# Splitting a weight block earlier, pinning its casts, and storing one output block in two parts, in a Strassen-Winograd MLP

## The chip, the cores and the metric

One core of a Trainium2 chip. The metric is the device time of one execution in microseconds (us). A kernel is quoted by the median of its timed executions; two kernels are compared by a ratio of executions made in the same rounds on the same chip. One profiled execution of each kernel gives its trace. That one execution need not be a median one.

The engines are named as in the profile: PE (matmul), PEld (weight load), DVE (VectorE), ACT (ScalarE), POOL (GpSimd) and SP (SyncE, which issues most of the DMAs).

## The reference

```python
# x: (8, 1024, 1024) f32, w1: (1024, 4096) f32, w2: (4096, 1024) f32
def reference(x, w1, w2):
    h = x @ w1
    h = 0.5 * h * (1 + np.tanh(np.sqrt(2 / np.pi) * (h + 0.044715 * h ** 3)))
    return (h @ w2).astype(np.float32)
```

## The kernel before

The 8192 rows of x go through in eight blocks of 1024 rows. Each block has a first product (x by w1, then gelu) and a second product (by w2). Both are done by Winograd's form of Strassen's algorithm: matrices are cut into quarters named 11, 12, 21, 22, and seven products of sums of quarters replace eight. All matmuls are f16, accumulated in f32. From the third block on ("steady" blocks) Strassen is applied twice for the second product, and for part of the first. The first two blocks apply it once, and use the time to make what the others need: the first block casts w1 and w2 from f32 to f16 and stores them to HBM, the second one makes the sums of quarters of quarters ("splits") and stores them too.

So three places matter here. **The first block's second product**, where quarters of w2 arrive in f32, are cast and used at once:

```python
# matmul2_made(sb, ...): second product of the first two blocks (cut)
def late_copy(out, in_):                  # cast on ACT, ordered behind the last gelu
    with tc.issue_after(gelu_last[0].ins):
        nc.scalar.copy(out=out, in_=in_)
...
bring("11", pool_copy, False)             # load w2 quarter 11, cast on POOL
bring("21", pool_copy, False)
bring("12", late_copy, True)              # 8 loads of 512 KB, 8 casts of 128x1024 on ACT
keep("11")                                # store the f16 form to HBM for later blocks
bring("22", late_copy, True)
for b in ("21", "12", "22"):
    keep(b)
...
for m, name, first in ((1, "a", True), (2, "b", True), (5, "c", True), (6, "a", False),
                       (3, "c", False), (7, "a", False), (4, "a", False)):
    for q in range(NQ):
        ...
        matmuls2(bank, s2[q] if m == 6 else rows(g[operands[m]], q), pieces(m), first)
        post(m, q, bank)                  # ACT copies or DVE adds of the bank
        if (m, q) == (2, 1) and sb == 0:
            xb = x_cast(sb + 1, at[1])    # cast of the next x by DMA on POOL's queue
        if (m, q) == ((5, 0) if sb else (6, NQ - 1)):
            xs = XOps(x_transpose(xb, load_in_order))   # transposes by DMA on SP's queue
        ...
        run((m, q))                       # DVE jobs of the table FILL, in program order
```

The table `FILL[sb]` says after which product (key `mq`) which DVE job is put: `g` sums of gelu's output, `w` sums of w2 quarters, `p1n` one sum of the split of quarter 11, `x` sums of the next x.

```python
slots("""10:g60;11:g61;12:g62;13:g63
;20:g50 w50 w51;21:g51 w52;22:w53 g52;23:g53 ...
```

**The second block's first product.** Its eight iterations j are one long stream of matmuls. The splits of raw quarters of w2 are made in it, two iterations for each quarter; they load halves of a quarter into buffers of a pool of four (`gcp`, "gc" in the trace), sum, and store:

```python
SPLIT_IN_M1 = (1, 2, 3)                   # quarters 11, 21, 22, named as in bring
...
if sb == 1 and j < 2 * len(SPLIT_IN_M1):
    m, h = SPLIT_IN_M1[j // 2], j % 2
    splits = split_in_m1(m, h)
...
def split_jobs(m, pieces):                # the other way to split, with whole u buffers
    def make(n):
        u, op, v = W_SUM[n]
        t[n] = unit(NI // 2, OH // 2)
        for h in range(2):
            tt(t[n][:, h * QC:(h + 1) * QC, :], operand(u, h), operand(v, h), op, True)
        nc.gpsimd.dma_start(out=in_d[m][:, SUMS.index(n)], in_=t[n])
```

**The seam between two steady blocks.** In the last product of a block (table `FILL_2`) the output quarters are put together. Quarter 22 gets two additions on DVE (`v`, `y`) before it is stored, and the block's last job (`i3`) makes four "inner sums" of the next x:

```python
;71:w11 w12;72:w21 w22;73:a37;74:a36 y11;75:a35 y12;76:a33 y21;77:y22
;31:z11 z12;32:z21 z22;33:v11 v12;34:v21 v22;36:n6;37:n3 i3
...
elif kind == "v":
    add(7, 5, b)
    if b[1] == "2":
        store_rows(sb, "22", m - 1, into[7][m - 1])
...
# next block's first product, iteration j (cut)
for h in range(2):
    add(a[h], banks_b[h])                 # this add releases PE
if sb > 1 and j == 0 and 3 not in xs.inner:
    xs.make_inner(3)                      # four sums of 128x512 f16, where i3 didn't make them
```

## Time and profile before

| | before |
|---|---|
| median of 3 executions | 1510.43 us (1510.37 to 1510.51) |
| the traced execution | 1513.48 us, span 1511.7, mean granted clock 0.996 |
| start of the first block's second product | 117.29 us |
| first block's second product | 102.93 us |
| second block's first product | 103.31 us |
| second block's second product | 96.69 us |
| six steady blocks, to PE's end | 1086.86 us |

The stages are read from the timeline of PE: from the first matmul of a stage to the first of the next. 448 matmuls of 128x512 at 0.2158 us are 96.7 us, so the second block's second product runs at full rate, and 102.93 and 103.31 hold some 6 us each of holes and slow clock. The traced execution is 3.05 us longer than the median.

How to read the lines below. A hole is a stretch in which PE is idle. In a timeline a line is: start, length, engine, line of the kernel, operation, output and input, form, number of instructions; the bracket at its end is the idle time before it and what ended it. In the windows view the columns are the window, its length, busy time (instructions) of PE, PEld, DVE, ACT and POOL, then the granted PE clock (1.00 is full speed), the DMA share and GB/s. SPq is the queue of the DMAs that SP issues. The prediction below shows most of the view of before. Two windows that it only tells of are these; the third figure from the end is the clock:

```profile
152.00:156.00 4.00, 3.93 (x11) 1.49 (x11) 4.00 (x6) 0.59 (x1) 0.79 (x2) 0.57 1.16 353
284.00:288.00 4.00, 3.38 (x10) 1.32 (x10) 4.00 (x7) 3.40 (x7) 1.23 (x3) 0.65 0.50 201
```

In both, PE gets through only ten or eleven matmuls in 3.93 and 3.38 us of busy time; at the full rate these would hold some 18 and 16.

### The profile page before, as it was taken

What the parts mean: (1) busy time and instruction counts of PE and PEld (TensorE: products, weight loads), DVE (VectorE), ACT (ScalarE), POOL (GpSimd) and SP (SyncE); (2) the same over time, 40 slices, a digit from 0 to 9 for tenths busy, and PEclk for the clock granted to TensorE, in tenths of its full rate; (3) what the DMA queues carried; (4) which work ended last, traced back from release to release, by engine and by line L of the source; (5) the groups of instructions that cost most, each with busy time, mean ns of one, the idle gap of its engine ahead of it and who ended that gap; (6) DMA issues with size and microseconds to landing.
All of it is one profiled execution on the core that took longest, in us unless ns stands there. A gap on an engine that the chain in (4) does not pass through costs nothing.

```text
span 1511.7 us, 26283 instructions
## 1 busy us (share of the span) xinstructions
PE 1483.2 (98%) x9839; PEld 959.9 (63%) x9839; DVE 1164.9 (77%) x1820; ACT 616.1 (41%) x1157; POOL 228.1 (15%) x315
## 2 busy tenths in 40 slices
PE   7999999999999999999999999999999999999998
PEld 3444444444455688557875588655886568855687
DVE  6654647758757799778997699867998779977788
ACT  5665116541056511664126631366214662156510
POOL 5551123312311011010111000110001101001010
PEclk9999999999999999999999999999999999999999
DMA  9999797999797898989989899898989999897894
GB/s 320 354 333 401 192 333 246 338 355 287 291 344 193 306 288 299 340 217 353 294 304 334 203 371 302 292 317 246 336 267 324 309 271 315 267 353 246 299 280 177
DMA packets 240095, 449.51 MB, mean 297 GB/s; under 512 B 80608, under 2 KB 85728, under 8 KB 239072
## 3 DMA queue, kind: packets, MB, share of 16 engines
q1 hardware_dynamic: 216256, 360.79, 71.3%
q0 software_dynamic: 23712, 87.05, 18.7%
q8 instruction: 77, 1.26, 0.3%
q14 instruction: 50, 0.41, 0.1%
HBM read 357.56 MB, written 104.86 MB: 306 GB/s over the span
## 4 chain that ended last, share of the span: by engine, by line
PE 83%; DVE 7%; DMA 5%; issue 3%; POOL 1%; ACT 0%; SPq 0%; DVEq 0%; POOLq 0%
PE ps L397 42%; PE ps L857 30%; PE ps L898 11%; DVE u L120 6%; DMA u<-in_w_dram 1%; DMA raw_d<-u 1%; DVE tmp L120 1%; DMA in_d<-gc 1%; DMA u<-in_x_dram 1%; DMA gc<-raw_d 1%; DVE gc L120 0%; DMA out_dram<-tmp 0%; POOL in_d L806 0%; SPq L133 0%; POOL w_d L214 0%
## 5 line engine op out<-in xcount | busy, mean ns | idle before, releaser
L397 PE MATMUL ps<-u 128*128 128x512 f16 (+1 forms) x4160 | 764.1, 346 | 16.4 <-DVE tmp L120 12.1
L120 DVE TENSOR_TENSOR tmp<-tmp,ps 128x256 f32<-128x256 f32 (+1 forms) x936 | 454.0, 533 | 274.8 <-PE ps L397 162.0
L397 PEld LDWEIGHTS <-u 128*128 128x128 f16 x4160 | 407.0, 98 | 369.9 <-issue 27.0
L136 ACT COPY tmp<-ps 128x512 f32<-128x512 f32 x416 | 235.1, 581 | 324.3 <-PE ps L397 160.9
L410 ACT ACTIVATE g<-tmp 128x512 f16<-128x512 f32 x384 | 241.7, 633 | 175.9 <-DVE tmp L120 175.7
L857 PE MATMUL ps<-u,gc 128*128 128x256 f16 x2688 | 300.4, 273 | 0.0
L857 PEld LDWEIGHTS <-gc 128*128 128x128 f16 x2688 | 262.5, 98 | 31.2
L120 DVE TENSOR_TENSOR u<-u 128x512 f32<-128x512 f32 (+3 forms) x312 | 235.2, 797 | 14.6 <-DMA u<-raw_d 8.9
L857 PE MATMUL ps<-u,g 128*128 128x256 f16 x2016 | 227.9, 273 | 0.0
L136 ACT COPY u<-ps 128x512 f32<-128x512 f32 (+1 forms) x136 | 78.8, 586 | 346.1 <-PE ps L857 341.5
L857 PEld LDWEIGHTS <-g 128*128 128x128 f16 x2016 | 197.3, 98 | 24.7
L898 PE MATMUL ps<-u,g 128*128 128x512 f16 x768 | 168.7, 382 | 3.9 <-DVE u L120 3.8
L120 DVE TENSOR_TENSOR u<-u,ps 128x512 f32<-128x512 f32 x216 | 147.4, 685 | 24.1 <-PE ps L857 18.5
L647 POOL DMA_DIRECT2D out_dram<-u x58 | 48.8, 884 | 731.2 <-DVE u L120 305.6
L898 PEld LDWEIGHTS <-g 128*128 128x128 f16 x768 | 75.5, 98 | 96.5 <-issue 5.7
L120 DVE TENSOR_TENSOR g<-g,g 128x2048 f16<-128x2048 f16 (+1 forms) x136 | 131.0, 986 | 1.6 <-ACT g L410 1.6
L120 DVE TENSOR_TENSOR gc<-g,gc 128x2048 f16<-128x2048 f16 x84 | 102.6, 1221 | 1.0 <-DVE gc L120 0.5
L120 DVE TENSOR_TENSOR gc<-g 128x2048 f16<-128x2048 f16 x78 | 95.2, 1221 | 0.0
L410 ACT ACTIVATE g<-ps 128x512 f16<-128x512 f32 x128 | 76.5, 597 | 10.1 <-PE ps L397 6.9
L139 POOL CAST u<-gc 128x1024 f16<-128x1024 f32 x40 | 47.9, 1207 | 40.5 <-DMA gc<-in_w_dram 36.2
L635 POOL DMA_DIRECT2D out_dram<-tmp x32 | 17.6, 550 | 110.6 <-DVE tmp L120 91.6
L494 POOL TENSOR_TENSOR gc<-g 128x2048 f16<-128x2048 f16 x6 | 24.4, 4064 | 63.2 <-ACT g L410 63.2
(33 smaller groups left out, 226.7 us busy)
## 6 DMA issues: line engine op xcount, KB each, us to landing
u<-w_d SPq DMA_DIRECT2D x336, 256.0 KB, 6.1
u<-in_d SPq DMA_DIRECT2D x168, 512.0 KB, 7.0
u<-raw_d SPq DMA_DIRECT2D x252, 256.0 KB, 7.0
out_dram<-u POOLq DMA_DIRECT2D x58, 512.0 KB, 7.1
gc<-in_w_dram SPq DMA_DIRECT2D x48, 512.0 KB, 6.0
u<-in_d SPq DMA_DIRECT2D x96, 256.0 KB, 6.7
raw_d<-u SPq DMA_DIRECT2D x32, 512.0 KB, 9.9
u<-raw_d SPq DMA_DIRECT2D x32, 512.0 KB, 11.8
```

The source lines that it names most:

```text
L120: i = nc.vector.tensor_tensor(out=out, in0=in0, in1=in1, op=op)
L136: tc.keep_in_program_order(nc.scalar.copy(out=out, in_=in_))
L139: pool_last[0] = nc.gpsimd.tensor_copy(out=out, in_=in_)
L397: tc.keep_in_program_order(nc.tensor.matmul(bank, lhsT=w, rhs=x, start=first and k == 0, stop=k == n - 1, skip_group_check=not first,))
L410: gelu_last[0] = nc.scalar.activation(out=g[b][:, c, :], in_=src, func=GELU)
L494: nc.gpsimd.tensor_tensor(out=early[7], in0=u, in1=v, op=SUB)
L635: return nc.gpsimd.dma_start(out=out2[r0:r0 + P, o0:o0 + OH], in_=src, **kw)
L647: return nc.gpsimd.dma_start(out=rows, in_=src, **kw)
L857: tc.keep_in_program_order(nc.tensor.matmul(bank[:, i * OH // 2:(i + 1) * OH // 2], lhsT=t[:, c, i * P:(i + 1) * P], rhs=self.y[j][:, c, : ...
L898: tc.keep_in_program_order(nc.tensor.matmul(pair(bank), lhsT=a[:, c, :], rhs=chunks(pieces[c // QC])[:, :, c % QC, :], start=(first and c ...
```

## The change

Its intent has four parts.

1. *Seams.* Quarter 22's second addition is made by an accumulating DMA: the first part is stored plainly, the second is added to it in HBM. The four inner sums are put behind the add that PE waits for.
2. *Casts.* The casts of w2's quarters 12 and 22 are pinned in program order on ACT; those of 22 come after the first product's copies.
3. *Split.* Quarter 11's split is made in the first block's second product, from pieces that are already in SBUF; the second block then makes two splits instead of three.
4. *Start.* The first cast of x is one DVE instruction instead of one on DVE and one on POOL, and some of the start's work is reordered.

```diff
-SPLIT_IN_M1 = (1, 2, 3)
+SPLIT_IN_M1 = (2, 3)
-    slots("""10:g60;11:g61;12:g62;13:g63
+    slots("""10:g60 p15;11:g61 p16;12:g62 p17;13:g63 p14
-    ;71:w11 w12;72:w21 w22;73:a37;74:a36 y11;75:a35 y12;76:a33 y21;77:y22
-    ;31:z11 z12;32:z21 z22;33:v11 v12;34:v21 v22;36:n6;37:n3 i3""")
+    ;71:y11 y12;72:y21 y22;73:a37;74:a36 w11;75:a35 w12;76:a33 w21;77:w22
+    ;31:z11 z12;32:z21 z22;36:n6;37:n3""")
 # ... make_inner becomes a list of jobs, inner_jobs ...
+            more = xs.inner_jobs(3) if j == 0 and sb > 1 and 3 not in xs.inner else []
                 elif start is None:
+                    for job in more[2 * h:2 * h + 2]:
+                        job()
                     five(h)
-            if sb > 1 and j == 0 and 3 not in xs.inner:
-                xs.make_inner(3)
 # ... the start's cast and order ...
-            for k in range(2):
-                cast = nc.vector.tensor_copy if k else nc.gpsimd.tensor_copy
-                tc.keep_in_program_order(cast(out=xn[:, k], in_=self.rows[a, q][:, k]))
+            tc.keep_in_program_order(nc.vector.tensor_copy(out=xn, in_=self.rows[a, q]))
 # ... matmul2_made ...
-        splits = {m: split_jobs(m, lambda m=m: sums[m]) for m in SUMS}
+        splits = {m: split_jobs(m, lambda m=m: pieces(m)) for m in (1, *SUMS)}
-        bring("12", late_copy, True)
+        bring("12", act_copy, True)
         keep("11")
-        bring("22", late_copy, True)
-        for b in ("21", "12", "22"):
-            keep(b)
+        if sb:
+            bring("22", None, False)
+                if (m, q) == (1, NQ - 1) and sb == 0:
+                    bring("22", act_copy, True)
+                    for b in ("21", "12", "22"):
+                        keep(b)
                 run((m, q))
 # ... matmul2 ...
+        products[7].rows = out("22", accum_op=ADD)
                 elif kind == "y":
                     add(5, 1, b)
+                    if b[1] == "2":
+                        store_rows(sb, "22", int(b[0]) - 1, into[5][int(b[0]) - 1])
-                elif kind == "v":
-                    add(7, 5, b)
-                    if b[1] == "2":
-                        store_rows(sb, "22", m - 1, into[7][m - 1])
```

More of the change, by code (lines that the diff above doesn't have):

```diff
@@ L57 @@
     ;61:n5;63:a77;64:a76;65:a75;66:a73;67:n7
-    ;71:w11 w12;72:w21 w22;73:a37;74:a36 y11;75:a35 y12;76:a33 y21;77:y22
-    ;31:z11 z12;32:z21 z22;33:v11 v12;34:v21 v22;36:n6;37:n3 i3""".replace("\n    ", ""))
+    ;71:y11 y12;72:y21 y22;73:a37;74:a36 w11;75:a35 w12;76:a33 w21;77:w22
+    ;31:z11 z12;32:z21 z22;36:n6;37:n3""".replace("\n    ", ""))
 @with_exitstack
@@ L281, in make_inner, with inner_jobs @@
         def make_inner(self, m):
+            for job in self.inner_jobs(m):
+                job()
+        def inner_jobs(self, m):
             self.inner[m] = up.tile([P, 4, 2, HT // 2], DT, name="u")
@@ L288, in operand @@
                 return self[m][:, 2 * k:2 * k + 2, t * HT // 2:(t + 1) * HT // 2]
-            for j, (u, op, v) in W_SUM.items():
-                tt(operand(j), operand(u), operand(v), op, True)
+            return [lambda j=j, s=s: tt(operand(j), operand(s[0]), operand(s[2]), s[1], True)
+                    for j, s in W_SUM.items()]
     def x_blocks():
@@ L318, in __init__ @@
                 self.load(1, q)
-            self.cast = self.quad.load_cols(1, 0, 2, (nc.gpsimd.tensor_copy, nc.scalar.copy))
+            self.cast = self.quad.load_cols(1, 0, 2, (nc.scalar.copy, nc.gpsimd.tensor_copy))
             for q in range(NQ):
@@ L516, in matmul1 @@
                 act_copy(a[h], banks_a[h])
-                if start is not None and j == 0:
-                    start.second(h)
             banks_c, p5, t = [], [], [temp(), temp()]
@@ L538, in matmul1 @@
                 elif start is None:
+                    for job in more[2 * h:2 * h + 2]:
+                        job()
                     five(h)
                 if start is not None and j == 0:
-                    start.second(2 + h)
+                    start.second(h)
             for _ in two:
                 pass
+            for q in range(2 if start is not None and j == 0 else 0):
+                start.second(2 + q)
             for h in range(2):
                 add(a[h], banks_b[h])
-            if sb > 1 and j == 0 and 3 not in xs.inner:
-                xs.make_inner(3)
             difference(j - 1)
@@ L653, in matmul2_made @@
         sums = {}
-        def late_copy(out, in_):
-            with tc.issue_after(gelu_last[0].ins):
-                nc.scalar.copy(out=out, in_=in_)
         def bring(b, cast, staged):
```

## The prediction

> **What bounds the kernel now.** I read the page first: who is busy, and what the chain of waits is made of.
>
> ```profile
> PE 1483.2 (98%) x9839; PEld 959.9 (63%) x9839; DVE 1164.9 (77%) x1820; ACT 616.1 (41%) x1157; POOL 228.1 (15%) x315
> ...
> PE 83%; DVE 7%; DMA 5%; issue 3%; POOL 1%; ACT 0%; SPq 0%; DVEq 0%; POOLq 0%
> ```
>
> PE is busy 98% of 1511.7 us, so at most 28.5 us of idle can be won, plus what a lowered clock costs. Next the timeline of PE alone: each line that ends in a bracket is a hole (idle before it, and its releaser).
>
> ```profile
> 21.76 5.31 PE L397 MATMUL ps<-u 128*128 128x512 f16 x16 [2.65 <-DVE u L120]
> ...
> 117.29 27.79 PE L898 MATMUL ps<-u,g 128*128 128x512 f16 x128
> 146.34 2.15 PE L898 MATMUL ps<-u,g 128*128 128x512 f16 x8 [1.26 <-DVE u L120]
> 150.34 1.02 PE L898 MATMUL ps<-u,g 128*128 128x512 f16 x4 [1.84 <-DVE u L120]
> 152.07 13.06 PE L898 MATMUL ps<-u,g 128*128 128x512 f16 x52 [0.71 <-DVE u L120]
> ...
> 284.62 26.02 PE L397 MATMUL ps<-u 128*128 128x512 f16 x112 [3.33 <-DVE tmp L120]
> 311.45 12.25 PE L397 MATMUL ps<-u 128*128 128x512 f16 x56 [0.81 <-DVE tmp L120]
> ...
> 604.58 4.28 PE L397 MATMUL ps<-u 128*128 128x256 f16 x26 [1.17 <-DVE tmp L120]
> 609.15 86.83 PE L397 MATMUL ps<-u 128*128 128x256 f16 x502 [0.29 <-DVE tmp L120]
> ```
>
> Full rate: 128 matmuls in 27.79 us, the last one 0.38 long, so (27.79 - 0.38)/127 = 0.2158 us from start to start. All holes are DVE arriving late. I then asked DVE and ACT around three of them. First block's second product (117 to 152 us), ACT, then DVE:
>
> ```profile
> 141.76 1.04 ACT L657 CAST u<-u 128x1024 f16<-128x1024 f32 x1 [0.19 <-DMA u<-in_w_dram]
> 142.71 2.04 ACT L136 COPY tmp<-ps 128x512 f32<-128x512 f32 x4
> ```
> ```profile
> 143.32 0.69 DVE L120 TENSOR_TENSOR tmp<-tmp,ps 128x512 f32<-128x512 f32 x1 [19.79 <-ACT tmp L136]
> ```
>
> The four copies of the first product's banks stand on ACT behind all sixteen casts of w2, the last eight of which wait for their loads. DVE sits idle 19.79 us for the first copy, then has everything at once, and PE waits for it. Second block (220 to 323 us), and the seam between two steady blocks:
>
> ```profile
> 283.27 0.69 DVE L120 TENSOR_TENSOR gc<-gc 128x1024 f16<-128x1024 f16 x1 [3.14 <-DMA in_d<-gc]
> ...
> 308.27 0.69 DVE L120 TENSOR_TENSOR gc<-gc 128x1024 f16<-128x1024 f16 x1 [4.87 <-DMA gc<-raw_d]
> ```
> ```profile
> 594.73 1.29 DVE L120 TENSOR_TENSOR u<-u 128x512 f32<-128x512 f32 x2
> ...
> 596.53 1.30 DVE L120 TENSOR_TENSOR u<-u 128x512 f32<-128x512 f32 x2
> ...
> 601.39 2.81 DVE L120 TENSOR_TENSOR u<-u 128x2048 f16<-128x2048 f16 x5
> 604.11 0.42 DVE L120 TENSOR_TENSOR tmp<-tmp,ps 128x256 f32<-128x256 f32 x1
> ```
>
> In the second block the DVE operations of the split sit in front of the adds that PE needs, and wait for DMA. At the seam DVE has not been idle since 582.9 us; the add that releases PE starts at 604.11 although its matmuls were done by about 602.3.
>
> **What the Trainium skill says.** "TensorE: Matmul & The Clock Gate", table "The two states you'll see": after an idle window of about 3.4 us PE runs at half rate, until a busy window of the same length. The trace agrees: in the windows view the granted clock is 0.57 in 152 to 156 us and 0.65 in 284 to 288, each after a long hole, and 1.00 at 600 to 604, after 1.17 us. The cost: 51 x 0.2158 + 0.38 = 11.39 us would be due for the 52 matmuls at 152.07; they took 13.06, so 1.67 lost; for the 112 at 284.62, 26.02 - 24.33 = 1.69. "DMA: Bandwidth & Descriptors", "Rules for kernel authors": an accumulating DMA must wait for the earlier write's semaphore, since nothing holds the bytes in between. The built kernel does wait so; no cost is seen in this trace, where block 11 is already stored like that. "SBUF — State Buffer", "SBUF: two separate sides": DVE and GpSimd share a port pair under an exclusive lock. The trace agrees: in the start DVE's 128x1024 sums take about 0.7 us alone, about 1.0 beside a POOL cast.
>
> **The change, part by part.** I compared the order of instructions of both builds on every engine. PE's matmuls are the same 9839, reordered only in the start.
>
> *Seams (plain plus accumulating stores; inner sums moved).* Four 128x512 f32 adds leave each of the six steady blocks (DVE 1822 to 1798 instructions). Back to back one takes 0.60 us: 2.4 us before each seam. Of the x5 at 601.39 the last four are inner sums of about 0.42 us; they move behind the add PE waits for: 1.7 us more. Redone with this: PE begins the block at 600.22; the last add of the old block needs its bank at about 600.4, so ends at 601.0; one 1.14 sum ends at 602.2; the releasing add runs 602.35 to 602.8. PE needs it after 12 x 0.2158 + 4 x 0.109 = 3.03 us, at 603.25. Slack 0.45 us, the hole closes. The moved sums, two and two, fit between later adds that wait for PE anyway. Worth 604.58 - 603.25 = 1.33 us at each of five seams: 6.65 us. The second hole of 0.29 us is set by ACT copy, adds and PE in turn, not by the backlog (it also stands at the second block's end, 427.81 us, where there is no backlog); it stays. The price is 1 MB more written per steady block, 6 MB beside 449.51, in a stretch (584 to 588 us) where the DMA share is 0.03. No PE hole in steady blocks waits for a load now.
>
> *w2 casts in program order.* ACT now does the eight casts of block 12, the four copies, then the eight casts of block 22. The first eight end about 127 us, the copies follow PE and end about 132. DVE's adds, at 0.69, and sums, at 1.22, then run with PE instead of after 143.3. From 117.29 to 178.78, the start of the next product, 256 matmuls should take 256 x 0.2158 = 55.24 us; they take 61.49. The 6.25 lost are 3.81 of holes, 0.5 of pipeline ends at three holes and 1.93 of slow clock. If DVE keeps up all of it comes back.
>
> *Split of 11 moved there.* DVE gets 8 more 128x1024 sums of about 0.72, 5.8 us, in time in which it idled 19.8 us: hidden. But they add four stores of 512 KB where the DMA share is 1.03 and 400 GB/s already run, about 5 us of DMA. And the fourth split job must wait for the third one's store to land, since it takes its buffer: the third is done about 126.5, landing takes 6 to 10 us, so DVE goes on at 133 to 137. Then the last sum that PE needs (w53) ends at about 144 to 148; PE needs it at 147.6. I charge 0.6. Block 22 comes about 5 us later, around 148 to 151; it is needed at about 156. Net of this and the part before: 6.25 - 0.6 = 5.65.
>
> In the second block the splits now fill iterations 1 to 4, not 1 to 6, so the hole at 311.45 goes: 0.81 + 0.17 of pipeline end = 1.0. Iterations 1 to 4 carry the same bytes in the same order as before, only of other blocks, so I let the hole at 284.62 (with its slow clock 5.2 us) stand.
>
> *Start.* DVE's cast of 1024 columns (mine: 0.43 + 0.26 = 0.69, the slope taken from 128x512 and 128x1024 f16 sums) replaces 0.43 on DVE beside 0.87 on POOL. The last cast ends 0.26 later, and everything to 29.4 us hangs on DVE. Against that, POOL's port is free for the first sums, about 0.3 us each for two of twelve. Net 0.
>
> *Tail.* Two 512 KB stores leave the last microseconds; the last store (3.3 us) may gain 0.2.
>
> Sum: 6.65 + 5.65 + 1.0 + 0 + 0.2 = 13.5. I take off 0.6 for waits I don't see: 12.9, or 1510.4 - 12.9 = 1497.5 us.
>
> **Rivals.** (1) The split's stores choke the DMA: for it, 400 GB/s and the buffer wait; against it, DVE's 19.8 idle us. It would leave 2 to 5 us of the first block's hole: about 1501. (2) The accumulating stores hold buffers and the DMA so that loads of the next block come late at each seam: for it, loads there already wait up to 8.7 us for stores; against it, the buffers of 22 are now stored 8 to 10 us earlier than before. With 1 us per seam gone: 1503 or more. (3) The hole at 284.62 depends on fine DMA timing and also goes: for it, it hangs on one 11.7 us store; against it, the same traffic. About 1492. (4) PE is bound by its own stream and nothing moves; against it, each hole names DVE as releaser: 1509.
>
> **Range and chances.** Mechanisms 1 and 2 are likely each on its own; 8 times in 10 between 1492.5 and 1503. All idle and slow clock together come to some 35 us, of which the change touches less than 20, so over 2% (30 us) faster is all but shut out; over 2% slower would need a new hole of 5 us in every steady block.
>
> **What would show it.** Right: no PE hole near 604 (and at the four other seams), the one near 609 still about 0.3; ACT's four tmp copies before 133 us and no DVE wait of 19.8 us; clock 1.00 after 145 us; the hole near 284 there, shifted by about 5.6 us, none near 311; first steady matmul stretch within 0.5 us of 27.5. Wrong: DVE waiting for a store of the split past 140 us; PE or DVE waiting for loads or stores at seams; a later start.

## The result, and the profile after

| | before | after |
|---|---|---|
| median of 4 executions of the same rounds | 1510.47 us (1510.37 to 1511.98) | 1501.02 us (1498.19 to 1501.52) |
| ratio after/before | | 0.9931 (0.9914 to 0.9948) |
| the traced execution | 1513.48 us, clock 0.996 | 1498.19 us, clock 0.999 |

A ratio here and below is the mean time of one kernel's executions over that of the other's executions of the same rounds, with its 95% interval; it is not quite the ratio of the medians. The change makes the kernel 0.7% faster, 9.45 us by the medians: within 2%, as predicted, and 3.5 us above the predicted time. The trace after is of the fastest of its four executions and the trace before is of one slower than the median, so the traces differ by 15.3 us. The stages:

| stage (us) | before | after | difference | predicted |
|---|---|---|---|---|
| to the first block's second product | 117.29 | 116.38 | 0.91 | 0 |
| first block's second product | 102.93 | 99.17 | 3.76 | 5.65 |
| second block's first product | 103.31 | 99.70 | 3.61 | 1.0 |
| second block's second product | 96.69 | 96.69 | 0 | 0 |
| six steady blocks | 1086.86 | 1079.78 | 7.08 | 6.65 |

The page of the kernel after has, in order, the busy times and the shares of the chain that ended last:

```profile
PE 1476.4 (99%) x9839; PEld 959.3 (64%) x9839; DVE 1154.8 (77%) x1796; ACT 616.4 (41%) x1157; POOL 236.1 (16%) x315
...
PE 87%; DMA 4%; issue 4%; DVE 2%; SPq 1%; POOL 1%; ACT 0%; POOLq 0%; DVEq 0%
```

PE is busy 6.8 us less with the same 9839 matmuls, so part of the gain is clock, not work. DVE's share of the chain fell from 7% to 2%. By the two pages the bytes written to HBM rose from 104.86 to 111.15 MB, the 6 MB that the plain stores cost.

Next PE's timeline of the kernel after, the lines that answer to the holes before:

```profile
116.38 41.60 PE L900 MATMUL ps<-u,g 128*128 128x512 f16 x192
157.82 2.75 PE L900 MATMUL ps<-u,gc 128*128 128x512 f16 x12
161.17 11.38 PE L900 MATMUL ps<-u,gc 128*128 128x512 f16 x52 [0.59 <-DVE u L120]
...
205.19 10.52 PE L900 MATMUL ps<-u,g 128*128 128x512 f16 x48 [1.56 <-DVE tmp L120]
...
279.00 36.42 PE L399 MATMUL ps<-u 128*128 128x512 f16 x168 [2.85 <-DVE tmp L120]
...
591.83 7.31 PE L399 MATMUL ps<-u 128*128 128x512 f16 x42
599.43 86.83 PE L399 MATMUL ps<-u 128*128 128x256 f16 x502 [0.29 <-DVE tmp L120]
```

The three holes of 3.81 us between 146 and 153 are gone: 192 matmuls from 116.38 run without a gap. Two new ones stand at 161.17 and 205.19. The hole of 3.33 us in the second block is now 2.85, at 279.00, and the one at 311 is gone. At the seam the 1.17 us hole is gone (its line at 604.58 in before) and the 0.29 one is still there.

ACT in the first block's second product, after:

```profile
127.51 1.55 ACT L136 COPY tmp<-ps 128x512 f32<-128x512 f32 x3
130.45 0.59 ACT L136 COPY tmp<-ps 128x512 f32<-128x512 f32 x1 [1.39 <-PE ps L900]
...
158.82 1.04 ACT L136 CAST u<-u 128x1024 f16<-128x1024 f32 x1 [8.18 <-DMA u<-in_w_dram]
```

The four copies are done at 131.04 instead of 144.75. But the last cast of quarter 22 comes at 158.82, because its load comes late. DVE in the first block, and in the second:

```profile
135.42 1.29 DVE L120 TENSOR_TENSOR u<-u 128x1024 f16<-128x1024 f16 x2 [9.18 <-DMA in_d<-u]
...
203.32 1.23 DVE L120 TENSOR_TENSOR u<-u 128x2048 f16<-128x2048 f16 x1 [5.96 <-DMA u<-raw_d]
...
277.65 0.69 DVE L120 TENSOR_TENSOR gc<-gc 128x1024 f16<-128x1024 f16 x1 [3.01 <-DMA in_d<-gc]
```

The first line is the split's fourth job waiting for a store of the split, as the prediction had it. The second is a w1 sum that waits for a load and stands in DVE's order before the add that PE wants at 205. The third is the wait behind the hole at 279. Last, DVE at the seam:

```profile
594.04 0.42 DVE L120 TENSOR_TENSOR tmp<-tmp,ps 128x256 f32<-128x256 f32 x1
594.50 0.88 DVE L120 TENSOR_TENSOR u<-u 128x512 f16<-128x512 f16 x2
```

The releasing add is now ahead of the inner sums, and starts 594.04 - 591.83 = 2.21 us after the block's first matmul; the prediction had 602.35 - 600.22 = 2.13.

And the clock. In the kernel after, the window behind the hole at 279 reads:

```profile
280.00:284.00 4.00, 4.00 (x21) 1.81 (x19) 4.00 (x8) 3.62 (x8) 1.62 (x3) 1.00 1.03 420
```

The hole of 2.85 us cost no clock in this execution.

### The profile page after: what moved, and what is told of

Same layout as the page of the kernel before. It is cut to its first block, busy times and chain, and to the rows that moved or that the text cites. A ratio compares the mean times of both kernels' runs of the same rounds, so it can differ in the third digit from the quotient of the medians.

```text
span 1496.4 us, 26271 instructions
## 1 busy us (share of the span) xinstructions
PE 1476.4 (99%) x9839; PEld 959.3 (64%) x9839; DVE 1154.8 (77%) x1796; ACT 616.4 (41%) x1157; POOL 236.1 (16%) x315
## 3 DMA queue, kind: packets, MB, share of 16 engines
q8 instruction: 77, 1.26, 0.3%
HBM read 355.47 MB, written 111.15 MB: 312 GB/s over the span
## 4 chain that ended last, share of the span: by engine, by line
PE 87%; DMA 4%; issue 4%; DVE 2%; SPq 1%; POOL 1%; ACT 0%; POOLq 0%; DVEq 0%
PE ps L399 45%; PE ps L859 34%; PE ps L900 7%; DVE tmp L120 1%; SPq L133 1%; DVE u L120 1%; DMA in_d<-gc 1%; DMA u<-in_x_dram 1%; DMA u<-raw_d 1%; DMA u<-in_w_dram 1%; DMA in_d<-u 1%; DMA xb<-in_x_dram 1%; POOL in_d L808 0%; POOL w_d L214 0%; POOL xb L371 0%
## 5 line engine op out<-in xcount | busy, mean ns | idle before, releaser
L120 DVE TENSOR_TENSOR u<-u 128x2048 f16<-128x2048 f16 (+3 forms) x296 | 225.6, 801 | 42.3 <-DMA u<-xb 13.4
L650 POOL DMA_DIRECT2D out_dram<-u x70 | 64.1, 988 | 710.1 <-issue 365.7
L376 POOL COPY pace<-g 128x2 f16<-128x2 f16 x24 | 4.5, 187 | 185.2 <-ACT g L412 185.2
```

The lines of the kernel that those rows point to most:

```text
L120: i = nc.vector.tensor_tensor(out=out, in0=in0, in1=in1, op=op)
L376: mark = nc.gpsimd.tensor_copy(out=pace, in_=g_chunk[:, :2])
L650: return nc.gpsimd.dma_start(out=rows, in_=src, **kw)
```

## The experiments

The questions: which part of the change gives what; why the first block's second product stayed 2.5 us above its ideal of 96.7; where the second block's extra gain came from. All twelve runs gave right results. Each ran beside executions of before: seams, casts, split and start (before: 1511.94); again, nosplit, xlate and spread (1511.36); p14_later, extra_stores and split_next (1510.68); timed_stores alone (1512.89).

| run | median us | ratio to before (95%) | first block's 2nd product | second block's 1st | steady |
|---|---|---|---|---|---|
| seams | 1504.51 | 0.9950 (0.9938 to 0.9962) | 99.55 | 103.79 | 1080.12 |
| casts | 1507.72 | 0.9972 (0.9960 to 0.9984) | 96.69 | 105.06 | 1086.89 |
| split | 1514.04 | 1.0022 (1.0009 to 1.0035) | 103.82 | 101.18 | 1087.02 |
| start | 1510.68 | 1.0003 (0.9984 to 1.0021) | 103.59 | 104.37 | 1087.11 |
| again | 1500.53 | 0.9929 (0.9913 to 0.9944) | 98.77 | 99.82 | 1079.81 |
| nosplit | 1501.66 | 0.9937 (0.9925 to 0.9949) | 96.70 | 104.11 | 1080.66 |
| xlate | 1502.80 | 0.9932 (0.9912 to 0.9952) | 102.07 | 103.20 | 1079.83 |
| spread | 1495.30 | 0.9897 (0.9884 to 0.9909) | 100.36 | 97.90 | 1080.05 |
| p14_later | 1501.34 | 0.9920 (0.9900 to 0.9940) | 100.73 | 101.47 | 1079.81 |
| extra_stores | 1501.26 | 0.9926 (0.9909 to 0.9943) | 96.69 | 104.58 | 1080.07 |
| split_next | 1495.37 | 0.9893 (0.9874 to 0.9912) | 96.70 | 97.71 | 1080.32 |
| timed_stores | 1501.55 | 0.9925 (0.9911 to 0.9938) | 97.35 | 102.64 | 1080.67 |

### seams: the seams alone

Before, with the changes of `FILL_2`, of `inner_jobs` and of the accumulating store only:

```diff
-    ;71:w11 w12;72:w21 w22;73:a37;74:a36 y11;75:a35 y12;76:a33 y21;77:y22
-    ;31:z11 z12;32:z21 z22;33:v11 v12;34:v21 v22;36:n6;37:n3 i3
+    ;71:y11 y12;72:y21 y22;73:a37;74:a36 w11;75:a35 w12;76:a33 w21;77:w22
+    ;31:z11 z12;32:z21 z22;36:n6;37:n3
+        products[7].rows = out("22", accum_op=ADD)
```

> Only the steady-block part (plain and accumulating stores of 22, inner sums behind the releasing add). Theory 'DVE backlog at five seams': 1.33 to 1.43 us at each, so 6.7 to 7.1 us faster than before, the holes of 1.17 us gone and those of 0.29 us left; first two blocks as before. Rival 'stores hold the DMA': less than 4 us faster, with loads or stores named as releasers at the seams.

Measured: 0.50% faster, 7.5 us of 1511. In the trace the steady blocks take 1086.86 - 1080.12 = 6.74 us less. PE's timeline at the same seam:

```profile
598.08 7.32 PE L401 MATMUL ps<-u 128*128 128x512 f16 x42
605.69 9.47 PE L401 MATMUL ps<-u 128*128 128x256 f16 x55 [0.29 <-DVE tmp L120]
```

The 42 matmuls run into each other where before had a hole of 1.17 us after 16 of them, and the 0.29 stays. So the seam part stands alone, and neither the extra bytes nor the later buffers take it back.

This trace shows one thing more. The code of the first block is that of before, but its second product takes 99.55 us, not 102.93. PE's timeline there:

```profile
149.51 1.02 PE L903 MATMUL ps<-u,g 128*128 128x512 f16 x4 [1.83 <-DVE u L120]
151.24 11.38 PE L903 MATMUL ps<-u,g 128*128 128x512 f16 x52 [0.71 <-DVE u L120]
```

The 52 matmuls behind nearly the same holes (1.83 and 0.71 us) take 11.38 us, the full rate; in the trace of before they took 13.06. Its first hole of 1.26 us is missing too. The start run, whose code there is the same again, took 103.59. So this stage varies by 4 us between executions without any change to it. Slow clock, which is missing in seams, makes 1.93 us in before and about 3 in start (8 matmuls in 2.99 us and 56 in 14.13); the rest is the length of the holes.

### casts: the pinned casts alone

```diff
-        bring("12", late_copy, True)
+        bring("12", act_copy, True)
         keep("11")
-        bring("22", late_copy, True)
-        for b in ("21", "12", "22"):
-            keep(b)
+        if sb:
+            bring("22", None, False)
+                if (m, q) == (1, NQ - 1) and sb == 0:
+                    bring("22", act_copy, True)
+                    for b in ("21", "12", "22"):
+                        keep(b)
```

> Only the pinned casts: block 22 brought after the first product, casts on ACT in program order; the split of 11 stays in the second block. Theory 'ACT head of line': no hole near 145, 3.5 to 6 us faster. Rival 'the earlier x cast takes it back': block 22's last load lands after 150 instead of 141.8 because the cast of x starts near 140 instead of 148.9, and holes of 0.5 to 2 us appear between 155 and 210; then only 2 to 4 us faster.

Measured: 0.28% faster, 4.2 us. PE's timeline:

```profile
158.31 13.98 PE L901 MATMUL ps<-u,gc 128*128 128x512 f16 x64
...
306.54 12.25 PE L397 MATMUL ps<-u 128*128 128x512 f16 x56 [2.66 <-DVE tmp L120]
```

The first block's second product is at its ideal, 96.69 us, without a hole: 6.24 us less than in before, against 6.25 in the prediction's working. That the copies stood behind the casts was the whole of that hole. The last cast of quarter 22 ended at about 141 us here, though the next x was being cast by DMA from about 140 on. But the second block's first product takes 105.06 us, 1.75 more than in before, with 2.66 us at 306.54 where before had 0.81. Seams and start, with the old code there, took 103.79 and 104.37 with holes of 1.48 and 2.30 us, so how much of this the casts make is open. And against the unchanged stage as seams and start show it (99.55 and 103.59), 96.69 is a gain of anything from 2.9 to 6.9 us. The times, 4.2 us, are the measure.

### split: the split alone

```diff
-SPLIT_IN_M1 = (1, 2, 3)
+SPLIT_IN_M1 = (2, 3)
-    slots("""10:g60;11:g61;12:g62;13:g63
+    slots("""10:g60 p15;11:g61 p16;12:g62 p17;13:g63 p14
-        splits = {m: split_jobs(m, lambda m=m: sums[m]) for m in SUMS}
+        splits = {m: split_jobs(m, lambda m=m: pieces(m)) for m in (1, *SUMS)}
```

> Only the split of 11 moved to the first block, casts unpinned as before. Theory 'the split only costs DMA there and frees the second block': second block 1 us (hole near 311) to 3.6 us (also the clock) shorter, first block 0 to 3 us longer since its four stores are in front of block 22's loads: between 2 us slower and 3 us faster in all. Rival 'hidden entirely': first block unchanged, 1 to 3.6 us faster.

Measured: 0.22% slower, 3.3 us, and the interval excludes zero; at most 2 us had been expected. PE's timeline:

```profile
150.52 3.59 PE L898 MATMUL ps<-u,g 128*128 128x512 f16 x8 [3.83 <-DVE u L120]
```

Without the pinned casts the copies still stand behind all sixteen casts. In before they started at 142.71, 25.42 us after the product's start; here 27.99 us after it, at 146.89, as the casts of quarter 22 wait longer for their loads, with the split's stores as new traffic beside them. The second block's first product gains 103.31 - 101.18 = 2.13 us in the traces, but the time as a whole is worse. So the split alone costs; with the casts pinned it costs nothing that the times show (nosplit, below).

### start: the start alone

```diff
-            for k in range(2):
-                cast = nc.vector.tensor_copy if k else nc.gpsimd.tensor_copy
-                tc.keep_in_program_order(cast(out=xn[:, k], in_=self.rows[a, q][:, k]))
+            tc.keep_in_program_order(nc.vector.tensor_copy(out=xn, in_=self.rows[a, q]))
 # and the order of second(h), and the engines of the second pair of w1 casts
```

> Only the start (x cast in one piece on DVE, order of the first products, ACT and POOL exchanged for one cast). Seen in the profile after: the start of the first block's second product came 0.9 us earlier. Theory 'port freed': 0.5 to 1.2 us faster. Rival 'DVE's longer cast': within 0.3 us of before, or slower.

Measured: 1.0003 (0.9984 to 1.0021), nothing that can be told from zero. Over all traces the first block's second product starts between 116.2 and 118.9 us, and the kernels with the new start (116.17 to 118.21) overlap with those without it (116.87 to 118.90). What the start is worth stays open: the interval of its ratio is some 3 us wide to either side. DVE's one-piece cast took 0.69 us, as worked out.

### again: the kernel after, unaltered

> The changed kernel once more, unaltered, to see how much its executions differ: the first four were 1498.2 and 1500.8 to 1501.5. Theory 'where transfers land relative to PE varies': the same program, in a trace nearer 1501, has its extra 3 us in the first two blocks (holes near 160, 205 or 279, or the lowered clock after one of them), the steady blocks the same to 0.3 us. Rival 'a slower clock everywhere': each steady block longer by 0.3 us or more.

Measured: 1500.53 us, from 1497.56 to 1504.96; its traced execution (1498.61 us) has the same holes as the first trace but the one at 161, 1.74 us at 205.62 and 2.93 at 279.54, and no slow clock after them. It is again a fast execution, so it does not show where the slow ones lose. The scatter goes with the mean granted clock. The ten executions of after, of both occasions:

| mean clock | executions | mean time, us |
|---|---|---|
| 0.999 | 2 | 1498.40 |
| 0.998 | 5 | 1499.82 |
| 0.997 | 1 | 1502.44 |
| 0.996 | 1 | 1504.96 |
| 0.995 | 1 | 1503.16 |

A fit gives 1.56 us per 0.001 of clock, and 0.001 of a 1500 us span is 1.5 us: the slow executions are, in the main, those in which PE runs slow for a while. The clock is not all of it, since the five at 0.998 still run from 1497.56 to 1501.52. Before does the same, less steeply (1510.6 us for six executions at 0.999, 1514.7 for five at 0.995). The start came at 117.21 us here, not at 116.38: the 0.91 us won at the start in the first trace is no property of the kernel. In that trace a hole of 0.43 us is missing that before has at 27.50 and again (0.47 us) at 27.42.

### nosplit: after, with the split taken back

```diff
-SPLIT_IN_M1 = (2, 3)
+SPLIT_IN_M1 = (1, 2, 3)
-    slots("""10:g60 p15;11:g61 p16;12:g62 p17;13:g63 p14
+    slots("""10:g60;11:g61;12:g62;13:g63
```

> The changed kernel with the split of 11 put back into the second block's first product. Theory 'the split is worth 1 to 3.6 us in the second block and costs up to 2 in the first': 0 to 3 us slower than the changed kernel. Rival 'its stores do harm': faster than the changed kernel.

Measured: 1501.66 us, beside 1500.53 for after: a difference of 1.1 us that lies within the scatter. Its stages tell more. The first block's second product is ideal (96.70), where after has 99.17 and 98.77: so the split costs 2.1 to 2.5 us there. The second block's first product takes 104.11, where after has 99.70 and 99.82: so the split gives 4.3 to 4.4 us there in these traces (p14_later and xlate, with slow clock in this stage, took 101.47 and 103.20). The hole near 279 is there without the split in the first block too, with 3.38 us at 279.24.

What stands between the split and the hole at 205 is seen on SP's queue. First after, then nosplit:

```profile
165.81 24.70 SPq L133 DMA_TRANSPOSE u<-xb  x16
```
```profile
162.25 24.58 SPq L133 DMA_TRANSPOSE u<-xb  x16
```

These sixteen transposes of the next x, and behind them in the same queue the loads of raw w1, are what DVE's in-order sums wait for. In after DVE waits for these transposes until 192.07 (8.60 us) and for such a load until 203.32 (5.96 us). Counted from the start of the product the transposes begin at 49.4 us in after and at 44.0 in nosplit. Part of the reason stands in the same queue: in front of them are the twelve stores of the f16 form of quarters 21, 12 and 22, and those of quarter 22 wait for its loads and casts. The last store is issued by 164.89 in after and by 161.12 in nosplit, 0.9 and 1.1 us before the first transpose. The next runs ask what delays it.

### xlate: the next x cast later

```diff
-                if (m, q) == (2, 1) and sb == 0:
-                    xb = x_cast(sb + 1, at[1])
+                if (m, q) == (2, NQ - 1) and sb == 0:
+                    xb = x_cast(sb + 1, at[NQ - 1])
```

> The changed kernel with the next block's x cast released by the store of the second product's last quarter, not its second: about 8 us later. Theory 'the cast of x takes DMA from block 22's loads': block 22's last load lands before 152 instead of 158.8, the holes at 161.17 (0.59) and 205.19 (1.56) vanish, 2 to 3 us faster than the changed kernel. Rival 'the split's stores delay block 22': holes stay, within 0.5 us of the changed kernel.

Measured: 1502.80 us; not faster than after. The idea held by half. PE, then two windows:

```profile
206.20 12.21 PE L900 MATMUL ps<-u,g 128*128 128x512 f16 x48 [3.53 <-DVE tmp L120]
```
```profile
206.00:210.00 4.00, 3.80 (x10) 1.41 (x10) 4.00 (x6) 0.00 (x0) 2.62 (x6) 0.57 1.03 423
282.00:286.00 4.00, 3.75 (x9) 1.32 (x9) 3.80 (x7) 3.77 (x8) 1.49 (x3) 0.50 1.03 421
```

Quarter 22's last cast is at 147.90 instead of 158.82 and the hole at 161 is gone: the cast of x does take DMA time from quarter 22's loads. But x then comes later, and the hole near 205 grows to 3.53 us. In this execution (1504.03 us, clock 0.995) the clock fell after it, and again after a hole of 3.07 us at 282. The steady stage is as in after (1079.83), so a slow execution is not slow everywhere: its loss sits behind these holes.

### p14_later: the split's fourth job out of the way

```diff
-    slots("""10:g60 p15;11:g61 p16;12:g62 p17;13:g63 p14
-    ;20:g50 w50 w51;21:g51 w52;22:w53 g52;23:g53
+    slots("""10:g60 p15;11:g61 p16;12:g62 p17;13:g63
+    ;20:g50 w50 w51;21:g51 w52;22:w53 g52;23:g53 p14
```

> The changed kernel with the fourth job of the split behind the last add of the second product, where it takes another buffer and waits for no store. Theory 'the added DMA bytes set the holes near 160 and 205': DVE's wait of 9.2 us for a store goes, the first block's second product and what follows takes 98.3 to 100.5 us as in the changed kernel (99.2 and 98.8 in two traces). Rival 'DVE's wait for the store sets them': 96.7 to 97.5 us, 2 us faster than the changed kernel.

Measured: 1501.34 us. DVE's wait of 9.18 us for the split's store is gone (its first add starts at 134.56, waiting for PE), but the hole near 205 is not:

```profile
205.70 12.21 PE L900 MATMUL ps<-u,g 128*128 128x512 f16 x48 [2.19 <-DVE tmp L120]
```

It is 2.19 us, and the 48 matmuls take 12.21 instead of 10.52: 1.69 of slow clock. So the wait that the prediction charged is not the one that costs. In this trace the cast of the next x is issued 23.1 us after the product's start, as in nosplit (25.8 in after), and the transposes are as late as in after, so a later cast of x is not what holds them up here.

### extra_stores: the split's bytes without its sums (failed as a test)

nosplit, with four stores of 512 KB to a spare buffer in HBM, at the places of the split's stores:

```diff
                 run((m, q))
+                if m == 1 and sb == 0:
+                    nc.gpsimd.dma_start(out=spare_d[:, q, :], in_=flat(raw["11"][q]))
```

> The changed kernel with the split of 11 back in the second block (as in nosplit, where the first block's second half took the ideal 96.70 us) plus four stores of 512 KB in the first block's first product that nothing reads and that need no work on DVE. Theory 'the bytes alone do it': 98.3 to 101 us there, with a hole near 205. Rival 'DVE's eight sums and the buffer do it': 96.7 to 97.2 us. Second block 103.5 to 105 us under both.

Measured: 1501.26 us, the first block's second product ideal (96.69). But the trace shows that the four stores were issued from 91.9 to 105.0 us, as soon as their data stood, ahead of the crowded stretch, and not at 120 to 137 as in after. So this run says nothing on the bytes.

### timed_stores: the same bytes at about the right time

nosplit, where each spare store reads a sum that is only made there:

```diff
                     tt(s2[n], rows(g["22"], n), rows(g["21"], n), SUB, True)
+                    if sb == 0:
+                        nc.gpsimd.dma_start(out=spare_d[:, n, :], in_=flat(s2[n]))
```

> As extra_stores, whose four stores left at 92 to 105 us, before the crowded stretch, and so tested nothing: here they carry what DVE makes at 118 to 123 us, so they leave there, as the split's do (120.7 to 137), with no work on DVE and no buffer that anybody waits for. Theory 'the bytes alone do it': the first block's second half takes 98.3 to 101 us (96.7 without them in nosplit), with a hole near 205 that a raw load and the transposes of x stand behind, transposes starting about 4 to 5 us later after that product's start than in nosplit (44.0). Rival 'DVE's sums and the buffer do it': 96.7 to 97.2 us, no hole near 205.

Measured: 1501.55 us. The four stores went out between 120.9 and 124.8 us (the split's in after between 120.7 and 137.5); quarter 22's last cast came at 157.35, as late as in after. The hole near 205 came back, but small:

```profile
204.77 10.52 PE L903 MATMUL ps<-u,g 128*128 128x512 f16 x48 [0.49 <-DVE tmp L121]
```

The product took 97.35 us. So bytes of this size at this time account for 0.65 of the 2.1 to 2.5 us. All runs with the pinned casts, by when SP was done issuing the transposes, counted from the product's start:

| run | casts | split_next | extra_stores | nosplit | timed_stores | again | p14_later | after | spread | xlate |
|---|---|---|---|---|---|---|---|---|---|---|
| transposes issued by, us | 66.1 | 66.9 | 68.3 | 68.6 | 71.7 | 73.7 | 74.0 | 74.1 | 75.2 | 75.4 |
| hole near 205, us | 0 | 0 | 0 | 0 | 0.49 | 1.74 | 2.19 | 1.56 | 2.11 | 3.53 |

Up to 68.6 us there is no hole, beyond 71 there is one, and it grows with few exceptions. The stores' bytes move the transposes by 3.1 us (68.6 to 71.7), the whole split by some 5.5. These are single traces, and the four without stores at that time differ by 2.5 us among themselves. The other 2.4 is not the buffer wait, which p14_later took away while the transposes stayed at 74.0; its sums, or which store meets which load, these runs do not separate.

### spread: the second block's two splits apart

after, with the four halves of the two splits spread over six iterations:

```diff
-SPLIT_IN_M1 = (2, 3)
+SPLIT_AT = {0: (2, 0), 2: (2, 1), 4: (3, 0), 5: (3, 1)}
-            if sb == 1 and j < 2 * len(SPLIT_IN_M1):
-                m, h = SPLIT_IN_M1[j // 2], j % 2
-                splits = split_in_m1(m, h)
+            if sb == 1 and j in SPLIT_AT:
+                splits = split_in_m1(*SPLIT_AT[j])
```

> The changed kernel with the remaining splits spread over iterations 1, 3, 5 and 6 of the second block, not 1 to 4, so that a buffer's store has an iteration more to land. Theory 'the hole at 279 is the split's own stores holding its buffers': that hole of 2.85 us goes (and its clock loss in runs that have it), 2.5 to 5 us faster than the changed kernel. Rival 'the DMA is full there anyway': the hole stays with a load as releaser, within 1 us.

Measured: 1495.30 us, ratio 0.9897; 5.2 us less than after in the same rounds. PE's timeline in the second block:

```profile
217.74 84.77 PE L399 MATMUL ps<-u 128*128 128x512 f16 x392
303.56 6.63 PE L399 MATMUL ps<-u 128*128 128x512 f16 x30 [1.05 <-DVE tmp L120]
```

392 matmuls in one piece where after stops for 2.85 us. Each half of a split takes two of the four `gc` buffers for what it loads and two for its sums, and those come free only when they are stored; that is the wait for `in_d<-gc` that DVE shows in after at 277.65. With an iteration or more between the halves the stores land in time. The last two halves still follow each other, and a hole of 1.05 us is left behind them; there DVE waits for a load of raw w2 (4.99 us, until 300.26). So the hole at 279 was made by the splits' own stores, one on the heels of the other. Of the 5.2 us the stages of the traces show only 1.8 to 1.9 (99.70 and 99.82 to 97.90). Both traces of after are of fast executions without slow clock behind this hole; that slow clock in the others makes the rest would fit p14_later and xlate, but is not shown.

### split_next: spread, and quarter 11's split in the second block

Quarter 11's split goes from the first block's table to the same places in the second block's (what the expectation calls split 12 is 21 in the code's names):

```diff
-    slots("""10:g60 p15;11:g61 p16;12:g62 p17;13:g63 p14     # first block
+    slots("""10:g60;11:g61;12:g62;13:g63
-    slots("""10:g60 w50;11:g61 w51;12:g62 w52;13:g63 w53     # second block
+    slots("""10:g60 w50 p15;11:g61 w51 p16;12:g62 w52 p17;13:g63 w53 p14
```

> An attempt to be better than all: splits of 12 and 22 spread as in spread, the split of 11 made in the second block's second product, off the first block. Expected from the stages: first block's second half 96.7, second block's first 97.9, its second 96.7 to 99, so 1 to 3.5 us faster than spread (1491 to 1495). Rival: DVE and DMA are full at the start of that product as well, and 2 to 6 us come back there; then no better than spread.

Measured: 1495.37 us, ratio 0.9893. PE's timeline of the second block's first product:

```profile
213.96 84.77 PE L399 MATMUL ps<-u 128*128 128x512 f16 x392
299.59 12.25 PE L399 MATMUL ps<-u 128*128 128x512 f16 x56 [0.86 <-DVE tmp L120]
```

The first block's second product has no hole at all, and both stages are near their ideal (96.70 and 97.71), and the second block's second product has room for the jobs: 96.69. The holes at 161 and 205 go when the split leaves the first block. The trace's span is 3.6 us under spread's, but the medians, from different calls, do not differ: with a stage gain of some 3.7 us one would expect more, and why the times do not show it is not known; spread's trace is of its slowest execution (1498.72 us), so part of that gain may not be in spread's usual executions at all. Both are 0.3 to 0.4% faster than after by the ratios, and about 1% faster than before.

## Why the prediction was right, and where its steps were off

The predicted time was 1497.5 us with a range from 1492.5 to 1503.0; the median is 1501.02, and 1500.53 when run again. Both forecasts, within 2% and the range, came true. By its steps:

1. *Seams, 6.65 us.* Right, in size and by its mechanism: 7.08 us in the trace of after, 6.74 in that of the part alone, 7.5 in the times of the part alone. The small hole of 0.29 us stayed, as said. The rival that the accumulating stores would take it back is refuted: the stores of this group landed in 9.3 us instead of 7.1 at the median, and no steady hole came of it (seams alone: 9.1 us). The two halves of this part were not run apart, and the trace of before says that the inner sums alone may do: an estimate from its lines is that without the four sums (about 1.7 us) the add of 604.11 starts at about 602.5 and ends by 603.0, before the 603.25 at which PE needs it. What the accumulating stores add to the gain is not shown.

2. *Casts, 6.25 us before the charge.* Right in the trace: casts alone took 6.24 us out of the first block's second product. Two things were missing. Of the 6.25, 1.93 us were slow clock, and the traced execution was one of before's slow ones (1513.48 us at clock 0.996; the median was 1510.43). The prediction took gains from that trace and subtracted them from the median. The seams run shows this stage, with the code of before, without any slow clock and 3.4 us shorter. How often before has the slow clock was not counted; that its median lacks part of it fits the other 42 executions of before (1512.6 us on average at clock 0.996, 1511.3 at 0.998, median clock 0.997), but no trace of a median execution was taken. And in casts the second block's first product was 0.7 to 1.75 us longer than in the three traces with the old code, which the prediction did not foresee.

3. *Split in the first block, charged 0.6 us.* This is the term that was mis-sized: it costs 2.1 to 2.5 us in the two traces of after, and more where its hole was longer or slow clock followed (4.0 in p14_later). The named mechanism did happen to the letter (the fourth job waited for a store until 135.42, predicted 133 to 137) and cost nothing: p14_later took the wait away and kept the hole. Quarter 22's last cast came at 158.82, not at 148 to 151, and made 0.59 us of hole at 161. The greater part came from where the prediction did not look: the split, in part by its stores, pushes back the next x's transposes and the raw loads behind them on SP's queue, and DVE's in-order sums that wait for those stand before an add that PE needs, some 70 us later. In its outcome this was the first rival, "the split's stores choke the DMA", for which the prediction gave 1501 us; but only about 0.65 us of it is shown to come from the stores' bytes.

4. *Second block, 1.0 us.* Too small: 3.6 us in the traces. The hole at 311 went as said (0.81 + 0.17). The rest: the hole at 284 lost 3.33 - 2.85 = 0.48, a hole of 0.31 us at 256.95 in before is gone, and 1.69 of slow clock that followed the hole in before did not follow it in after. The first two may be the split's or the trace's; the last comes and goes, as p14_later (1.46 us of slow clock after 2.76 of hole) and xlate (2.93 after 3.07) show beside after (none after 2.85). The third rival, that the hole at 284 goes as well, did not come true; spread shows what it would have taken, and that this is worth about 5 us in the times, of which the traces explain 1.9.

5. *Start, 0.* Nothing measurable, as said. One reading behind it was off: DVE's sums beside a POOL cast take 1.41 to 1.52 us in most cases in the trace of before, against 0.68 alone; 1.0 is the mean of all twelve. *Tail, 0.2.* From PE's end to the end of the span it is 4.62 us before and 4.68 after: nothing.

6. *The sum.* The casts' gain was taken some 2 us too large (4.2 in the times) and the split's cost there 1.5 to 1.9 us too small; the second block gave more, so the total came nearer than its parts. That is luck: errors of opposite sign. That the median meets the first rival's 1501 is in part luck too: the first block's loss is as that rival has it, the other terms are not. The 0.6 taken off "for waits I don't see" was of the right sign. The rival that nothing moves (1509) is refuted.

7. *The clock.* The prediction gave the clock of 600 to 604 us as the one after the hole of 1.17 us, but that hole runs from 603.41 to 604.58. The window behind it, 604 to 608, reads 1.00 as well, so the conclusion stands. And of the holes just before 152 none is longer than 1.84 us, so this trace does not agree with an idle window of 3.4 us as plainly as it says.

The parts alone sum to 7.5 + 4.2 - 3.3 - 0.5 = 7.9 us, and the whole gives 10.4 to 10.7 us by the two ratios: the difference is not clear of noise, since each part's interval is some 2 to 3 us wide to either side. The split may be part of it: alone it loses 3.3 us, on top of the pinned casts (nosplit to again) the medians gain about 1. After and nosplit are equal within the scatter, so the split as it was made brings little. Its place makes the holes at 161 and 205: in the second block's second product (split_next) it leaves neither, though the times of split_next and spread do not differ.

## What to carry to other kernels

Where an engine works in program order, look for what stands in front of the work that the bound engine waits for: taking casts off ACT's front, and inner sums and second additions off DVE's, gave nearly all of this gain (7.5 and 4.2 us alone). A move that is free for the engine it goes to can still be dear for the DMA queue: follow the queue's next hundred microseconds, not only the wait at the place of the move. And before a gain is read off one trace, compare that execution's time and mean clock with the median; slow clock in the trace may not be in the median, and cannot be won from it.

## What the Trainium skill lacked or had wrong

- "TensorE: Matmul & The Clock Gate", table "The two states you'll see": it puts the fall to half rate after an idle window of about 3.4 us, on a free-running window. Here much shorter holes were enough at times: 2.33 us in timed_stores and 2.19 us in p14_later each cost 1.69 us. Holes of 2.85 and 2.93 us (after, again) cost nothing, nor did one of 3.99 us (split: the 168 matmuls behind it took 36.42 us, the full rate). The length of a hole alone did not tell. A hole of 2 us and more should be told as a chance of slow clock, not as safe.
- The same page has half rate until a busy window of the same length, from which an estimate of the loss is 3.4 / 2 = 1.7 us. The runs agree for most spells (1.31 us in nosplit to 1.69 in before), but not for all: xlate lost 2.93 us after one hole, with clock 0.50 in one window of 4 us and 0.72 in the next. Its warm spacing of 215.7 ns agrees with 215.8 measured.
- The same part says that the count of slow matmuls at a kernel's start varies from run to run. What it lacks is that the same holds behind holes in the middle, and its size: 1497.6 to 1505.0 us for one kernel, 1.56 us per 0.001 of mean clock, and 52 matmuls in 13.06 us (before) or 11.38 us (seams) behind nearly the same holes (1.84 and 0.71 us, 1.83 and 0.71).
- "DMA: Bandwidth & Descriptors", "Rules for kernel authors": it says how an accumulating DMA has to be ordered, but not what it costs. Here 12 more stores of 512 KB in the same group, with as many of them now accumulating, raised the median from issue to landing from 7.1 to 9.3 us (9.1 in seams), and 6.29 MB more were written, without a new hole of PE in steady blocks.
- The same page, "Issuing engines are not separate DMA queues", says that DMAs of all engines share 16 DMA engines. The runs agree, with a size: four stores of 512 KB on POOL's queue put off the transposes on SP's queue by 3.1 us, some 40 us later (timed_stores against nosplit, single traces; runs without such stores differ by 2.5 us).
